# Low parts of weights written over the raw tiles in place, in a decoder trunk on one Trainium2 core

## The chip, the cores and the metric

The kernel runs on one core of one Trainium2 chip. The metric is device time in microseconds, lower is better; a run's time is that of the core. The engines named below are TensorE (PE, its weight loads PEld), VectorE (DVE), ScalarE (ACT), GpSimd (POOL) and SyncE (SP), which issues most DMA transfers.

## The reference

One layer of a decoder trunk on 256 positions of 2048 channels, in f32. The input is normalised, projected to seven widths of 1024 and three gates of 2048, and goes through three branches: a spatial-gating MLP (A), an S5 state-space layer with a GLU (B) and cross-attention into 256 memory tokens (X). Each is gated, projected back to 2048, weighed by a sigmoid gate and summed; an output projection, a norm and the residual follow.

```python
h = rms_norm(x, pre_g)
proj = h @ w_in
a_u, a_v, a_g, b_x, b_g, x_q, x_g, gate_logits = jnp.split(proj, splits, axis=-1)
y_a = spatial_gating(a_u, a_v, sg_ln_g, sg_ln_b, sg_w, sg_b) * jax.nn.silu(a_g)
y_b = s5_branch(b_x, ..., glu_w, glu_b) * jax.nn.silu(b_g)
y_x = memory_cross_attention(x_q, rms_norm(mem, mem_g), xa_wk, xa_wv) * jax.nn.silu(x_g)
branch = jnp.einsum('bsnc,ncd->bsnd', jnp.stack([y_a, y_b, y_x], axis=2), w_branch)
merged = jnp.sum(jax.nn.sigmoid(gate_logits) * branch, axis=2)
return x + rms_norm(merged @ w_out, post_g)
```

In the S5 branch the GLU is `y * sigmoid(y @ glu_w + glu_b)`, with `y` the GELU of the scan's output.

## The kernel before

Every large product is made of rounded f32 numbers in two parts: a weight `w` becomes a high part (a cast to the rounded type fp32r) and a low part (`w` minus the high part, rounded too), an activation likewise, and TensorE adds high x high, low x high and high x low. So each weight is loaded once, split once by a cast on ScalarE (L92) and a subtraction on VectorE (L93), and used by three groups of matmuls.

The weights come as 160 raw tiles of 128 partitions x 2048 f32 (1 MB each), numbered here from 0 in the order in which they are loaded: the S5 input (0 to 3), queries (4 to 11), keys, values, the X gate (28 to 35), the X merge with its gate logits and branch projection (36 to 59), A's three inputs, the A merge (84 to 107), B's gate (108 to 115), the gate logits of B (116 to 131), the GLU (132 to 135), the branch projection of B (136 to 143), and the output projection (144 to 159). A load is one DMA, issued by SP (`load`, L78), into one of three raw buffers. `split` (L85) cuts a tile in halves of 1024 columns: each takes one of four buffers `hl` of high and low part together. A raw buffer is free again when the second half has been subtracted, an `hl` buffer when TensorE has used it.

Two product forms use the tiles. `cm_block` has weights stationary (a tile is 16 blocks of 128 columns), `tm_quarter` has activations stationary and weights moving (a tile is 4 rows of 512). Results gather in two PSUM accumulators `acc`. An evacuation frees one: for the column form `fold` copies one half on ScalarE (L230) and adds the other on VectorE (L231). At the GLU (L904 to L919) a raw tile fills one accumulator, and its evacuation goes on with two sigmoids (ScalarE, L913), two products (VectorE, L915 and L916) and the split of two blocks `yB` (L92, L93), which the branch projection of B takes as stationary operand: tile 136 uses `yB` blocks 0 to 3, tile 137 blocks 4 to 7. In attention (L705 to L755), four heads share one PSUM buffer `misc` for scores `sc`, transposed probabilities `tp` (copied out by ScalarE, L734) and the output `po`.

The matmuls' order is the order in the code. The other engines get theirs from a scheduler, by due times and priorities: splits are raised by 250 steps (`AHEAD`), so that they come before evacuations; the S5 work (tables, scans, `E`, `p`, `s`) is fed in small steps between tiles by `pump`. Once built, each engine runs its list in order, and an instruction that waits holds all behind it.

Of the kernel before, what the change touches and what calls it, by code (L numbers as in the profile page):

```python
# [9 lines left out]
F32 = mybir.dt.float32  # L10
# [33 lines left out]
def trunk(ctx: ExitStack, tc: tile.TileContext, I, out):  # L44
    nc = tc.nc
    v, a, g, pe = nc.vector, nc.scalar, nc.gpsimd, nc.tensor

    xp = ctx.enter_context(tc.tile_pool(name="xp", bufs=1))
    xv = xp.tile([P, T + 48], F32, name="xv")
    const = ctx.enter_context(tc.tile_pool(name="const", bufs=1))  # L50
    big = ctx.enter_context(tc.tile_pool(name="big", bufs=1))
    rawp = ctx.enter_context(tc.tile_pool(name="rawp", bufs=3))
    hip = ctx.enter_context(tc.tile_pool(name="hip", bufs=4))
    wk = ctx.enter_context(tc.tile_pool(name="wk", bufs=2))
# [20 lines left out]

    def load(src):
        t = rawp.tile([P, 2048], F32, tag="raw", name=nm("raw"))
        nc.sync.dma_start(out=t, in_=src)  # L78
        return t

    def halves(off):
        t = hip.tile([P, 2 * 1024 + 128], F32R, tag="hl", name=nm("hl"))
        return t[:, off:off + 1024], t[:, off + 1024:off + 2048]

    def split(src, off=0):  # L85
        hi, lo = halves(off)
        with tc.high_priority(offset=AHEAD):
            split_to(hi, lo, src)
        return hi, lo
# [27 lines left out]
    const.tile([P, 32], F32, name="vpad")  # L117
    first = rawp.tile([P, 2, 768], F32, tag="raw", name="first", padded_shape=[P, 2, 1024])
    nc.sync.dma_start(out=xv, in_=I["xvecs"])
# [90 lines left out]
    def cm_block(ps, raw, hl, mm_=cm_mm):  # L210
        for hf in range(2):
            wh, wl = split(raw[:, hf * 1024:(hf + 1) * 1024], CM_OFF)
            for k in range(8):
                kk = hf * 8 + k
                mm_(ps, wh[:, k * P:(k + 1) * P], wl[:, k * P:(k + 1) * P], hl[kk], kk == 0, kk == 15)
            pump(rate["cm"])

    def tm_quarter(acc, raw, hl, kq, nk):
        for hf in range(2):
            wh, wl = split(raw[:, hf * 1024:(hf + 1) * 1024])  # L220
            for k in range(2):
                kk = kq * 4 + hf * 2 + k
                sl = slice(k * 512, (k + 1) * 512)
                for tb in range(2):
                    tm_mm(acc[tb], wh[:, sl], wl[:, sl], hl[kk], tb, kk == 0, kk == nk - 1)
            pump(rate["tm"])

# [6 lines left out]
    def cm_pairs(src, nblk, hl, evac, mm_=cm_mm):  # L234
        for bp in range(nblk // 2):
            ps = acc_tile()
            for b in range(2):
                cm_block(ps[:, b], load(src[2 * bp + b]), hl, mm_)
            evac(bp, ps)
# [10 lines left out]
    for pc in range(8):  # L250
        if pc == 0:
            raw = first
        elif pc < 3:
            raw = rawp.tile([P, 2, 768], F32, tag="raw", name=nm("st"), padded_shape=[P, 2, 1024])
        else:
            raw = slot(("H0", "H1", "H2", "H3", "M0")[pc - 3], [P, 2, 1024])[:, :, 0:768]
        wh, wl = (z.rearrange("p (q n) -> p q n", q=2) for z in halves(CM_OFF))
        parts = [slice(0, 1), slice(1, 2)]
        for q in parts if pc < 3 else [slice(0, 2)]:
            if pc > 0 or q.start > 0:  # L260
                nc.sync.dma_start(out=raw[:, q], in_=I["start"][pc][:, q])
# [509 lines left out]
    def merge(n, yhl, sink):  # L771
        for c in range(4):
# [212 lines left out]
    for kh in range(2):  # L985
        raw = load(I["w_out3"][0, kh])
        for hf in range(2):
            wh, wl = split(raw[:, hf * 1024:(hf + 1) * 1024])
            for k in range(4):
                for tb in range(2):  # L990
                    tm_k(acc[:, tb, 0:T], wh[:, k * T:(k + 1) * T], wl[:, k * T:(k + 1) * T], kh * 8 + hf * 4 + k, tb)
    for tb in range(2):
# [8 lines left out]
    for kh in range(2):  # L1001
        raw = load(I["w_out3"][1, kh])
        for hf in range(2):
            src = raw[:, hf * 1024:(hf + 1) * 1024]
            if kh == 0 and hf == 0:
                for i in range(2):
                    wh = s5p.tile([P, 512], F32R, tag="s", name=nm("wh"), bufs=4)
                    wl = s5p.tile([P, 512], F32R, tag="s", name=nm("wl"), bufs=4)
                    split_to(wh, wl, src[:, i * 512:(i + 1) * 512])
                    wks += [(wh[:, k * T:(k + 1) * T], wl[:, k * T:(k + 1) * T]) for k in range(2)]  # L1010
            else:
                wh, wl = split(src)
                wks += [(wh[:, k * T:(k + 1) * T], wl[:, k * T:(k + 1) * T]) for k in range(4)]
    at = [bup.tile([P, 512], F32, tag="bu", name=nm("oacc")) for _ in range(2)]
# [115 lines left out]
```

## Time and profile before

| | |
|---|---|
| median of 3 runs | 914.53 us (914.26 to 915.4) |
| the profiled execution | 915.75 us, of which 914.0 us lie between first and last instruction |
| granted TensorE clock | 0.999 |
| TensorE, VectorE, ScalarE busy | 900.7, 765.3, 560.0 us |
| HBM read, written | 190.39 MB, 2.10 MB (211 GB/s over the span) |

In rows of the profile a line like L93 is that of the helper; `hl` is a high and low buffer, `raw` a raw tile, `acc` an accumulator. A row of a group ends in its busy time and the mean of one, and after the second bar the idle time of the engine before these instructions, with what ended it. A row of the timeline begins with start and duration in us. A row of the waits gives the total, the number of times and the longest. Engines other than TensorE have idle time that costs nothing.

### The profile page before, as it was taken

What the parts mean: (1) busy time and instruction counts of PE and PEld (TensorE: products, weight loads), DVE (VectorE), ACT (ScalarE), POOL (GpSimd) and SP (SyncE); (2) the same over time, 40 slices, a digit from 0 to 9 for tenths busy, and PEclk for the clock granted to TensorE, in tenths of its full rate; (3) what the DMA queues carried; (4) which work ended last, traced back from release to release, by engine and by line L of the source; (5) the groups of instructions that cost most, each with busy time, mean ns of one, the idle gap of its engine ahead of it and who ended that gap; (6) DMA issues with size and microseconds to landing.
All of it is one profiled execution on the core that took longest, in us unless ns stands there. A gap on an engine that the chain in (4) does not pass through costs nothing.

```text
span 914.0 us, 12943 instructions
## 1 busy us (share of the span) xinstructions
PE 900.7 (99%) x4864; PEld 798.7 (87%) x4864; DVE 765.3 (84%) x1202; ACT 560.0 (61%) x962; POOL 22.4 (2%) x46
## 2 busy tenths in 40 slices
PE   8999999999999999999999999999999999999996
PEld 6999898889888888889999888888988889998896
DVE  6899967976779999999888799999997967876554
ACT  7575755755558677666454765777666647544452
POOL 1000000000000000000000000000000000000000
PEclk9999999999999999999999999999999999999999
DMA  9887565555454565655755556556655565657542
GB/s 350 303 309 295 219 231 190 196 189 191 147 205 167 200 232 211 235 188 189 257 182 207 177 176 223 186 199 222 213 190 210 195 236 203 216 185 276 197 172 93
DMA packets 30175, 193.33 MB, mean 212 GB/s; under 512 B 3744, under 2 KB 4128, under 8 KB 8352
## 3 DMA queue, kind: packets, MB, share of 16 engines
q1 hardware_dynamic: 28000, 186.08, 56.7%
q0 software_dynamic: 1536, 4.20, 1.4%
q10 hardware_dynamic: 576, 2.23, 0.7%
q8 instruction: 38, 0.62, 0.3%
q14 instruction: 25, 0.20, 0.1%
HBM read 190.39 MB, written 2.10 MB: 211 GB/s over the span
## 4 chain that ended last, share of the span: by engine, by line
PE 74%; DVE 17%; ACT 3%; issue 3%; DMA 1%; SPq 0%; DVEq 0%; ACTq 0%
PE acc L175 17%; PE acc L180 15%; PE acc L181 15%; PE acc L182 15%; PE acc L174 8%; DVE hl L93 6%; DVE p L371 2%; ACT hl L92 2%; DVE p L600 1%; DVE s L371 1%; PE y L624 1%; PE po L742 1%; DMA M<-memT 1%; DMA st<-start 1%; DVE q L371 1%
## 5 line engine op out<-in xcount | busy, mean ns | idle before, releaser
L93 DVE TENSOR_TENSOR hl<-raw,hl 128x1024 fp32r<-128x1024 f32 x319 | 388.6, 1221 | 112.0 <-ACT hl L92 110.5
L92 ACT CAST hl<-raw 128x1024 fp32r<-128x1024 f32 x319 | 330.7, 1045 | 200.0 <-PE acc L182 120.8
L175 PE MATMUL acc<-x,hl 128*128 128x512 f32 x736 | 241.6, 383 | 0.1
L174 PE MATMUL acc<-x,hl 128*128 128x256 f32 x690 | 189.1, 274 | 1.4 <-DVE hl L93 1.4
L180 PE MATMUL acc<-hl,x 128*128 128x512 f32 x448 | 171.5, 383 | 0.0
L181 PE MATMUL acc<-hl,x 128*128 128x512 f32 x448 | 169.9, 379 | 0.8 <-DVE hl L93 0.8
L182 PE MATMUL acc<-hl,x 128*128 128x512 f32 x448 | 169.8, 379 | 0.0
L175 PEld LDWEIGHTS acc<-x,hl 128*128 128x128 f32 x736 | 137.0, 190 | 18.1 <-ACT hl L92 1.0
L174 PEld LDWEIGHTS acc<-x,hl 128*128 128x128 f32 x690 | 132.3, 192 | 3.0 <-DVE hl L93 1.7
L180 PEld LDWEIGHTS acc<-hl,x 128*128 128x128 f32 x448 | 84.7, 189 | 14.1 <-issue 2.9
L181 PEld LDWEIGHTS acc<-hl,x 128*128 128x128 f32 x448 | 84.7, 189 | 12.4 <-DVE hl L93 1.2
L182 PEld LDWEIGHTS acc<-hl,x 128*128 128x128 f32 x448 | 84.7, 189 | 12.0
L180 PE MATMUL acc<-hl,H 128*128 128x512 f32 (+1 forms) x224 | 83.5, 373 | 0.0
L181 PE MATMUL acc<-hl,H 128*128 128x512 f32 (+1 forms) x224 | 83.2, 372 | 0.0
L182 PE MATMUL acc<-hl,H 128*128 128x512 f32 (+1 forms) x224 | 83.2, 372 | 0.0
L175 PE MATMUL acc<-H,hl 128*128 128x512 f32 x192 | 62.6, 382 | 0.0
L174 PE MATMUL acc<-H,hl 128*128 128x256 f32 x176 | 48.2, 274 | 0.2 <-DVE hl L93 0.2
L182 PEld LDWEIGHTS acc<-hl,H 128*128 128x128 f32 x224 | 42.4, 189 | 5.6
L181 PEld LDWEIGHTS acc<-hl,H 128*128 128x128 f32 x224 | 42.4, 189 | 5.4
L180 PEld LDWEIGHTS acc<-hl,H 128*128 128x128 f32 x224 | 42.4, 189 | 5.3
L371 DVE TENSOR_TENSOR p<-bu,E 128x512 f32<-128x512 f32 x64 | 41.9, 686 | 0.9 <-PE bu L562 0.7
L600 DVE TENSOR_TENSOR_SCAN p<-s5r,p 128x256 f32<-128x256 f32 x64 | 40.9, 680 | 0.6
(253 smaller groups left out, 1187.4 us busy)
## 6 DMA issues: line engine op xcount, KB each, us to landing
raw<-w_gate SPq DMA_DIRECT2D x48, 1024.0 KB, 4.8
raw<-w_br SPq DMA_DIRECT2D x24, 1024.0 KB, 4.7
raw<-w_out SPq DMA_DIRECT2D x16, 1024.0 KB, 4.8
raw<-w_xq SPq DMA_DIRECT2D x8, 1024.0 KB, 4.9
raw<-wk SPq DMA_DIRECT2D x8, 1024.0 KB, 4.7
raw<-wv SPq DMA_DIRECT2D x8, 1024.0 KB, 4.8
raw<-w_xg SPq DMA_DIRECT2D x8, 1024.0 KB, 4.7
raw<-w_av SPq DMA_DIRECT2D x8, 1024.0 KB, 4.8
```

What stands on the lines that cost most here:

```text
L92: a.copy(out=hi, in_=src)
L93: v.tensor_tensor(out=lo, in0=src, in1=hi.bitcast(F32), op=ALU.subtract)
L174: pe.matmul(ps[:, 0:T], lhsT=wl, rhs=hl.moving(0), start=False, stop=False)
L175: pe.matmul(ps, lhsT=wh, rhs=hl.moving_both(), start=first, stop=last)
L180: pe.matmul(ps, lhsT=hl.stationary(0, tb), rhs=two(wh), start=first, stop=False)
L181: pe.matmul(ps, lhsT=hl.stationary(0, tb), rhs=two(wl), start=False, stop=False)
L182: pe.matmul(ps, lhsT=hl.stationary(1, tb), rhs=two(wh), start=False, stop=last)
L371: v.tensor_tensor(out=o, in0=i0, in1=i1, op=op)
L600: v.tensor_tensor_scan(out=p2[:, ri], data0=rb, data1=p1[:, ri], initial=0.0, op0=ALU.mult, op1=ALU.add)
L624: pe.matmul(ps[32 * j:32 * j + 32, :], lhsT=cbt[:, cb * 4 + j, ri, :], rhs=ss[j][:, ri, :], start=ri == 0, stop=ri == 1, tile_position=(0, ...
L742: pe.matmul(po[:, c, :], lhsT=vv[:, mb, (2 * h + c) * P:(2 * h + c + 1) * P], rhs=pT[:, h, mb, :], start=mb == 0, stop=mb == 1)
```

## The change

A raw tile now becomes its own low part. There are four buffers, each seen by two names, `raw` (f32) and `low` (fp32r), at one address; three `hl` buffers hold the 2048 high columns of a whole tile. `split` makes two casts of 1024 columns, as before, and then one subtraction of 2048 columns that writes the low part over the raw tile. So a raw buffer is free when TensorE has used it, and SP's loads wait for TensorE where they waited for VectorE. In column form a tile is placed 352 bytes further in, as the `hl` buffers were. The start pieces use the same buffers; their splits keep their sizes. The gate sigmoids `sg` of the merges move from a work pool to free slots (X0, H0). The last output tile, whose first half was split in quarters into small buffers, is split like the others. What each product computes is the same.

```diff
--- before.py
+++ after.py
@@ -35,6 +35,8 @@
 BEHIND = 0
 NWARM = 8
 CM_OFF = 352 // 4
+NRAW = 4
+RW = 2048 + 128
 RT = (0.66, 0.8, 0.47, 0.62, 0.58, 0.55, 1.32)
 GELU_S = 2.0 * math.sqrt(2.0 / math.pi)
 GELU_C = 0.044715
@@ -45,12 +47,16 @@
     nc = tc.nc
     v, a, g, pe = nc.vector, nc.scalar, nc.gpsimd, nc.tensor
 
+    at0 = nc.sbuf_base
+    nc.alloc_sbuf_tensor("arena", [P, NRAW * RW + 128], F32)
+    at0 += (320 - at0) % 512
+    raws = [nc.alloc_sbuf_tensor_at(f"raw{i}", [P, RW], F32, offset=at0 + i * RW * 4).ap() for i in range(NRAW)]
+    lows = [nc.alloc_sbuf_tensor_at(f"low{i}", [P, RW], F32R, offset=at0 + i * RW * 4).ap() for i in range(NRAW)]
     xp = ctx.enter_context(tc.tile_pool(name="xp", bufs=1))
     xv = xp.tile([P, T + 48], F32, name="xv")
     const = ctx.enter_context(tc.tile_pool(name="const", bufs=1))
     big = ctx.enter_context(tc.tile_pool(name="big", bufs=1))
-    rawp = ctx.enter_context(tc.tile_pool(name="rawp", bufs=3))
-    hip = ctx.enter_context(tc.tile_pool(name="hip", bufs=4))
+    hip = ctx.enter_context(tc.tile_pool(name="hip", bufs=3))
     wk = ctx.enter_context(tc.tile_pool(name="wk", bufs=2))
     s5p = ctx.enter_context(tc.tile_pool(name="s5p", bufs=2))
     s5c = ctx.enter_context(tc.tile_pool(name="s5c", bufs=1))
@@ -73,19 +79,32 @@
         s = nm("sm")
         return const.tile(shape, dt, tag=s, name=s)
 
-    def load(src):
-        t = rawp.tile([P, 2048], F32, tag="raw", name=nm("raw"))
-        nc.sync.dma_start(out=t, in_=src)
-        return t
+    turn = [0]
+
+    def next_raw():
+        turn[0] += 1
+        return (turn[0] - 1) % NRAW
+
+    def load(src, off=0):
+        i, sl = next_raw(), slice(off, off + 2048)
+        nc.sync.dma_start(out=raws[i][:, sl], in_=src)
+        return raws[i][:, sl], lows[i][:, sl], off
+
+    def high(off):
+        return hip.tile([P, RW], F32R, tag="hl", name=nm("hl"))[:, off:off + 2048]
 
     def halves(off):
-        t = hip.tile([P, 2 * 1024 + 128], F32R, tag="hl", name=nm("hl"))
-        return t[:, off:off + 1024], t[:, off + 1024:off + 2048]
-
-    def split(src, off=0):
-        hi, lo = halves(off)
+        t = high(off)
+        return t[:, 0:1024], t[:, 1024:2048]
+
+    def split(raw):
+        src, lo, off = raw
+        hi = high(off)
         with tc.high_priority(offset=AHEAD):
-            split_to(hi, lo, src)
+            for hf in range(2):
+                sl = slice(hf * 1024, (hf + 1) * 1024)
+                a.copy(out=hi[:, sl], in_=src[:, sl])
+            v.tensor_tensor(out=lo, in0=src, in1=hi.bitcast(F32), op=ALU.subtract)
         return hi, lo
 
     def split_to(hi, lo, src):
@@ -115,7 +134,10 @@
     a.activation(out=warm, in_=warm, func=AF.Exp)
     vecs = xv[:, T:T + 48]
     const.tile([P, 32], F32, name="vpad")
-    first = rawp.tile([P, 2, 768], F32, tag="raw", name="first", padded_shape=[P, 2, 1024])
+    def raw_piece():
+        return raws[next_raw()][:, 0:1536].rearrange("p (q n) -> p q n", q=2)
+
+    first = raw_piece()
     nc.sync.dma_start(out=xv, in_=I["xvecs"])
     nc.scalar.dma_start(out=first[:, 0, T:T + 256], in_=I["start"][0][:, 0, T:T + 256])
     nc.sync.dma_start(out=first[:, 0, T + 256:768], in_=I["start"][0][:, 0, T + 256:768])
@@ -208,22 +230,21 @@
     rate = {"cm": 0.62, "tm": RT[6]}
 
     def cm_block(ps, raw, hl, mm_=cm_mm):
-        for hf in range(2):
-            wh, wl = split(raw[:, hf * 1024:(hf + 1) * 1024], CM_OFF)
-            for k in range(8):
-                kk = hf * 8 + k
-                mm_(ps, wh[:, k * P:(k + 1) * P], wl[:, k * P:(k + 1) * P], hl[kk], kk == 0, kk == 15)
-            pump(rate["cm"])
+        wh, wl = split(raw)
+        for k in range(16):
+            mm_(ps, wh[:, k * P:(k + 1) * P], wl[:, k * P:(k + 1) * P], hl[k], k == 0, k == 15)
+            if k % 8 == 7:
+                pump(rate["cm"])
 
     def tm_quarter(acc, raw, hl, kq, nk):
-        for hf in range(2):
-            wh, wl = split(raw[:, hf * 1024:(hf + 1) * 1024])
-            for k in range(2):
-                kk = kq * 4 + hf * 2 + k
-                sl = slice(k * 512, (k + 1) * 512)
-                for tb in range(2):
-                    tm_mm(acc[tb], wh[:, sl], wl[:, sl], hl[kk], tb, kk == 0, kk == nk - 1)
-            pump(rate["tm"])
+        wh, wl = split(raw)
+        for k in range(4):
+            kk = kq * 4 + k
+            sl = slice(k * 512, (k + 1) * 512)
+            for tb in range(2):
+                tm_mm(acc[tb], wh[:, sl], wl[:, sl], hl[kk], tb, kk == 0, kk == nk - 1)
+            if k % 2:
+                pump(rate["tm"])
 
     def fold(ps, bc):
         t = wk.tile([P, 2, T], F32, tag="w0", name=nm("f"))
@@ -235,7 +256,7 @@
         for bp in range(nblk // 2):
             ps = acc_tile()
             for b in range(2):
-                cm_block(ps[:, b], load(src[2 * bp + b]), hl, mm_)
+                cm_block(ps[:, b], load(src[2 * bp + b], CM_OFF), hl, mm_)
             evac(bp, ps)
 
     wz = wk.tile([P, 512], BF16, tag="w1", name="wz", padded_shape=[P, 1024])
@@ -251,7 +272,7 @@
         if pc == 0:
             raw = first
         elif pc < 3:
-            raw = rawp.tile([P, 2, 768], F32, tag="raw", name=nm("st"), padded_shape=[P, 2, 1024])
+            raw = raw_piece()
         else:
             raw = slot(("H0", "H1", "H2", "H3", "M0")[pc - 3], [P, 2, 1024])[:, :, 0:768]
         wh, wl = (z.rearrange("p (q n) -> p q n", q=2) for z in halves(CM_OFF))
@@ -776,7 +797,9 @@
                 tm_quarter([G[:, 0], G[:, 1]], load(I["w_gate"][n, c, kq]), xhl, kq, 16)
             assert not bg[2]
             Bp = acc_tile()
-            sg = wk.tile([P, 2, 512], F32, tag="w0", name=nm("g"))
+            if c == 0:
+                sgs = slot("X0" if n == 2 else "H0", [P, 2, 2, 512])
+            sg = sgs[:, c % 2]
             for tb in range(2):
                 a.activation(out=sg[:, tb], in_=G[:, tb], func=AF.Sigmoid, scale=rstd_x[:, tb:tb + 1])
             for kq in range(2):
@@ -903,9 +926,9 @@
         yB += [s5p.tile([P, 2, T], F32R, tag=tag, name=nm("yB"), bufs=n) for _ in range(n)]
     for bp in range(4):
         ps = acc_tile()
-        raw = load(I["glu"][bp])
+        gh, gw = (z.rearrange("p (b n) -> p b n", b=2) for z in split(load(I["glu"][bp], CM_OFF)))
         for b in range(2):
-            wh, wl = split(raw[:, b * 1024:(b + 1) * 1024], CM_OFF)
+            wh, wl = gh[:, b], gw[:, b]
             for k in range(8):
                 cm_mm(ps[:, b], wh[:, k * P:(k + 1) * P], wl[:, k * P:(k + 1) * P], ygl[k], k == 0, k == 7)
         t = fold(ps, None)
@@ -999,18 +1020,8 @@
 
     wks = []
     for kh in range(2):
-        raw = load(I["w_out3"][1, kh])
-        for hf in range(2):
-            src = raw[:, hf * 1024:(hf + 1) * 1024]
-            if kh == 0 and hf == 0:
-                for i in range(2):
-                    wh = s5p.tile([P, 512], F32R, tag="s", name=nm("wh"), bufs=4)
-                    wl = s5p.tile([P, 512], F32R, tag="s", name=nm("wl"), bufs=4)
-                    split_to(wh, wl, src[:, i * 512:(i + 1) * 512])
-                    wks += [(wh[:, k * T:(k + 1) * T], wl[:, k * T:(k + 1) * T]) for k in range(2)]
-            else:
-                wh, wl = split(src)
-                wks += [(wh[:, k * T:(k + 1) * T], wl[:, k * T:(k + 1) * T]) for k in range(4)]
+        wh, wl = split(load(I["w_out3"][1, kh]))
+        wks += [(wh[:, k * T:(k + 1) * T], wl[:, k * T:(k + 1) * T]) for k in range(8)]
     at = [bup.tile([P, 512], F32, tag="bu", name=nm("oacc")) for _ in range(2)]
     ro = small([P, 2])
     ms = small([P, 2])
...
```

The hunks left out give the column loads of `w_bx` their offset and write the output projection's split as one call for a tile.

The matmuls stand in the same order. On VectorE 1202 instructions become 1042, and what stands between them moves. VectorE at the GLU, before: the sum of an accumulator (L231) for tile 132, half subtractions of the next tiles (`hl`), products, and the `yB` low parts.

```order
L93 TENSOR_TENSOR hl_7231<-raw_7210,hl_7231 128x1024
L231 TENSOR_TENSOR f_7146<-acc_7105,f_7146 128x512
L93 TENSOR_TENSOR hl_7264<-raw_7262,hl_7264 128x1024
L915 TENSOR_TENSOR f_7146<-f_7146,U_129 128x512
L916 TENSOR_TENSOR f_7146<-f_7146,X_788_5937 128x512
L93 TENSOR_TENSOR hl_7283<-raw_7262,hl_7283 128x1024
L93 TENSOR_TENSOR yB_7097<-f_7146,yB_7097 128x256
L93 TENSOR_TENSOR yB_7098<-f_7146,yB_7098 128x256
L231 TENSOR_TENSOR f_7198<-acc_7157,f_7198 128x512
```
The same place now (L252 is the sum, L107 the subtraction of a whole tile, L938 and L939 the products, L112 the `yB` low parts; `low_61` is tile 135, `low_62` tile 136):

```order
L107 TENSOR_TENSOR low_61<-raw_57,hl_6854 128x2048
L252 TENSOR_TENSOR f_6743<-acc_6705,f_6743 128x512
L938 TENSOR_TENSOR f_6743<-f_6743,U_133 128x512
L939 TENSOR_TENSOR f_6743<-f_6743,X_564_5609 128x512
L107 TENSOR_TENSOR low_62<-raw_58,hl_6903 128x2048
L112 TENSOR_TENSOR yB_6697<-f_6743,yB_6697 128x256
L112 TENSOR_TENSOR yB_6698<-f_6743,yB_6698 128x256
L252 TENSOR_TENSOR f_6792<-acc_6754,f_6792 128x512
```
Before, `raw_7262` is tile 135: the sum of tile 132 stood ahead of its two halves and that of tile 133 right behind them. Now the sum of tile 132 has all of tile 135 ahead of it, and that of tile 133 all of tile 136.

ScalarE there, before, from the second cast of tile 135 on:

```order
L92 CAST hl_7283<-raw_7262 128x1024
L92 CAST yB_7097<-f_7146 128x256
L92 CAST yB_7098<-f_7146 128x256
L230 COPY f_7198<-acc_7157 128x512
L92 CAST hl_7316<-raw_7314 128x1024
L913 ACTIVATE f_7198<-f_7198,xv 128x256 x2
L92 CAST hl_7331<-raw_7314 128x1024
```
And now, from the casts of tile 136 on:

```order
L106 CAST hl_6903<-raw_58 128x1024 x2
L111 CAST yB_6697<-f_6743 128x256
L111 CAST yB_6698<-f_6743 128x256
L251 COPY f_6792<-acc_6754 128x512
L106 CAST hl_6932<-raw_55 128x1024 x2
L936 ACTIVATE f_6792<-f_6792,xv 128x256 x2
L251 COPY f_6841<-acc_6803 128x512
```
The copy of tile 133's accumulator (`f_7198`) stood ahead of the first cast of tile 136 (`raw_7314`), the sigmoids between that tile's two casts; now the copy (`f_6792`) stands behind both casts of tile 136, and its sigmoids behind both of tile 137.

ScalarE in attention, between the copy of the S5 base `E` and the copy of the first head's transposed probabilities `tp`, before:

```order
L541 COPY E_2644<-ebase 128x2x32
L549 ACTIVATE t_2650<-E_2644,pwr 128x32
L550 ACTIVATE t_2650<-E_2644,pwr 128x32
L92 CAST hl_2084<-raw_2060 128x1024
L230 COPY f_1995<-acc_1884 128x512
L734 COPY H_195_1883<-tp_1988 128x512
```
And now:

```order
L562 COPY E_2520<-ebase 128x2x32
L570 ACTIVATE t_2526<-E_2520,pwr 128x32
L106 CAST hl_2020<-raw_58 128x1024 x2
L251 COPY f_1907<-acc_1802 128x512
L755 COPY H_137_1801<-tp_1900 128x512
```
Between the two copies stood one cast of a weight and now there are two.

More of the change, by code (lines that the diff above doesn't have):

```diff
@@ L345, in trunk @@
     b45 = [bup.tile([P, 512], F32, tag="bu", name=f"bx{i}") for i in (4, 5)]
-    cm_block(b45[0], load(I["w_bx"][0]), xhl)
+    cm_block(b45[0], load(I["w_bx"][0], CM_OFF), xhl)
     for i in range(2):
         fold_u(u[:, 2 * i:2 * i + 2, :], acc0[i])
-    cm_block(b45[1], load(I["w_bx"][1]), xhl)
+    cm_block(b45[1], load(I["w_bx"][1], CM_OFF), xhl)
     ps = acc_tile()
-    cm_block(ps[:, 0], load(I["w_bx"][2]), xhl)
+    cm_block(ps[:, 0], load(I["w_bx"][2], CM_OFF), xhl)
     for i in range(2):
@@ L356, in trunk @@
         nc.sync.dma_start(out=Cin[i], in_=I["s5c"][:, i])
-    cm_block(ps[:, 1], load(I["w_bx"][3]), xhl)
+    cm_block(ps[:, 1], load(I["w_bx"][3], CM_OFF), xhl)
     fold_u(u[:, 6:8, :], ps)
@@ L985, in trunk @@
     for kh in range(2):
-        raw = load(I["w_out3"][0, kh])
-        for hf in range(2):
[L988 to L991, printed above, removed]
+        wh, wl = split(load(I["w_out3"][0, kh]))
+        for k in range(8):
+            for tb in range(2):
+                tm_k(acc[:, tb, 0:T], wh[:, k * T:(k + 1) * T], wl[:, k * T:(k + 1) * T], kh * 8 + k, tb)
     for tb in range(2):
@@ L1001, in trunk @@
     for kh in range(2):
-        raw = load(I["w_out3"][1, kh])
-        for hf in range(2):
-            src = raw[:, hf * 1024:(hf + 1) * 1024]
-            if kh == 0 and hf == 0:
-                for i in range(2):
-                    wh = s5p.tile([P, 512], F32R, tag="s", name=nm("wh"), bufs=4)
-                    wl = s5p.tile([P, 512], F32R, tag="s", name=nm("wl"), bufs=4)
-                    split_to(wh, wl, src[:, i * 512:(i + 1) * 512])
-                    wks += [(wh[:, k * T:(k + 1) * T], wl[:, k * T:(k + 1) * T]) for k in range(2)]
-            else:
-                wh, wl = split(src)
-                wks += [(wh[:, k * T:(k + 1) * T], wl[:, k * T:(k + 1) * T]) for k in range(4)]
+        wh, wl = split(load(I["w_out3"][1, kh]))
+        wks += [(wh[:, k * T:(k + 1) * T], wl[:, k * T:(k + 1) * T]) for k in range(8)]
     at = [bup.tile([P, 512], F32, tag="bu", name=nm("oacc")) for _ in range(2)]
```

## The prediction

> **What bounds the kernel now.** I read the page's busy lines first, then its chain, then the groups, then the list of waits.
>
> ```profile
> PE 900.7 (99%) x4864; PEld 798.7 (87%) x4864; DVE 765.3 (84%) x1202; ACT 560.0 (61%) x962; POOL 22.4 (2%) x46
> PE 74%; DVE 17%; ACT 3%; issue 3%; DMA 1%; SPq 0%; DVEq 0%; ACTq 0%
> L93 DVE TENSOR_TENSOR hl<-raw,hl 128x1024 fp32r<-128x1024 f32 x319 | 388.6, 1221 | 112.0 <-ACT hl L92 110.5
> L92 ACT CAST hl<-raw 128x1024 fp32r<-128x1024 f32 x319 | 330.7, 1045 | 200.0 <-PE acc L182 120.8
> L175 PE MATMUL acc<-x,hl 128*128 128x512 f32 x736 | 241.6, 383 | 0.1
> ```
>
> TensorE is busy 99% of the 914.0 us and almost never waits. The weight splits (L93, L92) are the largest groups of VectorE and ScalarE, yet both engines wait there for work: ScalarE 120.8 us for a matmul that frees a buffer, VectorE 110.5 us for ScalarE's cast. Only what stops TensorE can be won, and the list of waits has nearly all of it:
>
> ```profile
> PEld acc L174 <- DVE hl L93: 2.5, 3, 1.7
> PE acc L174 <- DVE hl L93: 1.6, 2, 1.4
> PE sc L711 <- ACT H L734: 1.4, 1, 1.4
> PE acc L181 <- DVE hl L93: 0.8, 1, 0.8
> ...
> 10.25 0.38 PE L174 MATMUL acc<-x,hl 128*128 128x256 f32 x1 [1.44 <-DVE hl L93]
> 99.59 0.38 PE L175 MATMUL acc<-H,hl 128*128 128x512 f32 x1
> 100.15 0.38 PE L174 MATMUL acc<-H,hl 128*128 128x256 f32 x1 [0.17 <-DVE hl L93]
> 609.83 0.38 PE L180 MATMUL acc<-hl,x 128*128 128x512 f32 x1
> 610.98 0.48 PE L181 MATMUL acc<-hl,x 128*128 128x512 f32 x1 [0.77 <-DVE hl L93]
> ```
>
> The list's 1.4 us of L174 lie at 10.25 us, before the first weights, in the start pieces, whose splits keep their sizes; they stay. The other places show how late a matmul starts: with 0.22 us from one matmul of 512 columns to the next, 100.15 is 0.34 late and 610.98 is 0.93 late, and the scores of L711 wait 1.4. That is 2.7 us; with the short pauses within 1 us of them I put what a faster split could win at 3.5 us at the most (an estimate).
>
> **The change, part by part.**
>
> *Fewer, longer subtractions.* 319 of 1024 columns become 160 of 2048. No row has 2048 columns; bounds come from these:
>
> ```profile
> 30.46 2.36 DVE L93 TENSOR_TENSOR hl<-raw,hl 128x1024 fp32r<-128x1024 f32 x2 [0.26 <-ACT hl L92]
> L371 DVE TENSOR_TENSOR p<-bu,E 128x512 f32<-128x512 f32 x64 | 41.9, 686 | 0.9 <-PE bu L562 0.7
> ```
>
> Above: two alone, 2 x 1.221 = 2.44 us. Below: 686 ns at 512 and 1221 at 1024 make 535 ns for each 512, so 1.221 + 1.070 = 2.29 us. I take 2.29. Per tile VectorE gains 0.15 us against separate halves, but 0.07 against the back-to-back pair of the row (2.36); over 160 tiles that is 11 to 24 us of its 765, on an engine which is idle 16% of the span. On TensorE's path that gain is worth nothing: the cover is the 5.2 us that one tile's matmuls take (below). Without that cover it would be up to 0.15 us a tile.
>
> [...]
>
> *Buffers and loads.* A raw tile is now freed by the last matmul on it, not by its second subtraction. Four buffers let the load of a tile start when TensorE ends the fourth tile before it.
>
> ```profile
> raw<-w_gate SPq DMA_DIRECT2D x48, 1024.0 KB, 4.8
> 777.33 0.38 PE L180 MATMUL acc<-hl,yB 128*128 128x512 f32 x1
> 780.35 0.38 PE L182 MATMUL acc<-hl,yB 128*128 128x512 f32 x1
> 782.51 0.38 PE L180 MATMUL acc<-hl,yB 128*128 128x512 f32 x1
> ```
>
> A tile lasts 782.51 - 777.33 = 5.18 us, so the load has three tiles, 15.5 us, less 4.8 to land. The high buffer (three now) comes free two tiles ahead, 10.4 us; two casts (2 x 1.045) and one subtraction (2.29) take 4.4, so both halves are ready about 6.0 us early. In steady state nothing stalls, and SP's loads standing behind a matmul cost 0. Where VectorE was backlogged by the state-space work (94 to 100 and 611 us), its order now puts that tile's subtraction several us of work earlier, so I take its 1.3 us of lateness (0.34 + 0.93) with the pauses beside it: -2.0 (bounds 0, and -2.1 of the 3.5 once the 1.4 of the scores is out).
>
> *Evacuations stand behind whole tiles.* ScalarE and VectorE run in program order, and splits are put ahead of the rest. Where an evacuation used to come between two halves, it now waits for two casts (2.1 us) and then for 2.29 us, not for half of each. Most have a tile or two of slack. At the GLU and the projection after it they have none. VectorE, ScalarE and TensorE of before there:
>
> ```profile
> 761.81 1.05 ACT L92 CAST hl<-raw 128x1024 fp32r<-128x1024 f32 x1 [1.53 <-PE acc L175]
> 762.76 0.58 ACT L230 COPY f<-acc 128x512 f32<-128x512 f32 x1
> 765.38 0.90 ACT L913 ACTIVATE f<-f,xv 128x256 f32<-128x256 f32 x2
> 768.15 0.71 ACT L92 CAST yB<-f 128x256 fp32r<-128x256 f32 x2
> 767.37 0.69 DVE L916 TENSOR_TENSOR f<-f,X 128x512 f32<-128x512 f32 x1
> 770.00 0.68 DVE L231 TENSOR_TENSOR f<-acc,f 128x512 f32<-128x512 f32 x1
> 774.53 0.76 DVE L93 TENSOR_TENSOR yB<-f,yB 128x256 fp32r<-128x256 f32 x2
> 784.94 0.75 DVE L93 TENSOR_TENSOR yB<-f,yB 128x256 fp32r<-128x256 f32 x2
> 771.87 0.60 PE L175 MATMUL acc<-H,hl 128*128 128x512 f32 x2
> 785.53 0.38 PE L182 MATMUL acc<-hl,yB 128*128 128x512 f32 x1
> ```
>
> Tile numbers count loads: 132 to 135 are the GLU, 136 and 137 the first projection tiles. I play the new order by hand on the old TensorE clock, with these durations. Tile 135 starts at 772.09 (the second matmul of the 771.87 row) if the sum of tile 133's accumulator (L231, ended 770.68) has freed it: 1.4 us of slack. Now: casts of 135 end at 763.8, its subtraction at 766.1, the sum of 132 at 766.7, the sigmoids at 767.6, the two products at 769.05; casts of 136 to 769.6, its subtraction to 771.9, two yB subtractions to 772.5, and only then the sum of 133, to 773.15. Tile 135 starts at 773.2: **+1.1**. Next: casts of 137 to 774.3, sigmoids of 133, copy of 134 to 775.6, subtraction of 137 to 776.6, product, sum of 134 and product to 778.35, its sigmoids to 778.7, its products to 780.15; casts of 138 to 780.7, subtraction to 782.95, first yB low of block 2 at 783.3. Tile 136, started at 778.45, wants it 780.35 - 777.33 = 3.02 us in, at 781.5: **+1.8**. It ends at 785.45, which frees the buffer for tile 139's casts (to 787.8); the subtraction ends at 790.05 and the yB low of block 6 at 790.4. Tile 137 wants that at 785.45 + 3.02 = 788.5: **+1.9**. Sum **+4.8 us**. In the old trace the same operand was ready about 785.35 for a matmul at 785.53, so almost no slack was there. Bounds: 0, if every added wait falls into slack, and 6.8, three times one more cast and half subtraction (3 x 2.27).
>
> *Attention.* The second scores wait for one PSUM buffer, which ScalarE's copy of the transposed probabilities frees.
>
> ```profile
> 188.53 1.22 DVE L93 TENSOR_TENSOR hl<-raw,hl 128x1024 fp32r<-128x1024 f32 x1
> 191.26 0.68 DVE L371 TENSOR_TENSOR s<-p,E 128x512 f32<-128x512 f32 x1
> 191.98 0.25 ACT L541 COPY E<-ebase 128x64 f32<-128x64 f32 x1 [3.10 <-DVE s L371]
> 192.69 1.03 ACT L92 CAST hl<-raw 128x1024 fp32r<-128x1024 f32 x1
> 194.11 0.58 ACT L734 COPY H<-tp 128x512 f32<-128x512 f32 x1
> 194.74 2.00 PE L711 MATMUL sc<-M,X 128*128 128x256 f32 x8 [1.42 <-ACT H L734]
> ```
>
> Before, one cast stood between the E copy and that copy; now two do (+0.95), and the E copy waits for an `s` product that stands behind a whole subtraction (+1.0, less what the two half ones around it gave back). The copy ends near 196.4 and the scores start 1.7 us later: **+1.7** (bounds -0.2, if the relieved VectorE is early, and +2.1, a cast and half a subtraction). The other three heads have slack of about what one cast adds: 0.
>
> *The rest.* The sigmoid gates move to free slots of the same form, and the last projection tile no longer splits in quarters; both end well before TensorE wants them: 0. Start and tail keep their work: 0.
>
> *Sum.* 915.75 (the profiled execution, 1.75 around its span) - 2.0 + 4.8 + 1.7 = 920.25. The median of the runs shown is 1.2 under the profiled time, so I predict **919.0 us**.
>
> **The rivals.**
>
> *No change.* The GLU slack absorbs the order: ScalarE's queue shifts so that evacuations run in the 1.53 us idle spells, as the row at 761.81 shows one. Then -2.0 and about +2 swap: 914.5. For it: both engines are idle often. Against it: the order is fixed, an idle spell before a cast can't be used by a sum behind it.
>
> *Faster.* VectorE is what matters wherever it is the releaser (17% of the chain). Its 11 to 24 us come off ahead of the stalled places, the three stalls go whole (-3.5) and the GLU sums still arrive inside their 1.4 us: 914.53 - 3.5 + at most 1 = 911.0 to 912.0. It decides if the chain of sums at the GLU comes out 1 us earlier than played. [...] Against it: the subtraction before a sum is longer than the old half by 1.07 us, five times in a row.
>
> *Slower still.* Loads wait for matmuls, and where extra megabytes share the queue the lead goes:
>
> ```profile
> M<-memT SPq DMA_DIRECT2D x2, 1024.0 KB, 7.5
> M<-mem SPq DMA_DIRECT2D x2, 1024.0 KB, 6.7
> ACT wh L92 <- DMA raw<-w_out: 0.8, 1, 0.8
> ```
>
> With one such megabyte ahead the landing takes 4.8 + 7.5 = 12.3 of the 15.5 us, leaving 3.2 where the two casts and the subtraction want 4.4: 1.2 us late against the first matmul, up to four times between 37 and 90 us. It decides from a landing of 11.1 us on. Then 919.0 + 3 to 5 = 922 to 924. Against it: the waits of before have no load as releaser of a weight cast beyond one of 0.8 us.
>
> **How the numbers follow.** This kernel's measurement can't tell a change within 0.2%, or 1.8 us. My forecast (916.4 to 921.5) has 0.50, no change 0.25 (912.7 to 916.4), faster 0.13, slower still 0.12. So faster 0.13, same 0.25, slower 0.62. The likeliest case's own range is 916.4 to 921.5; the range for 8 in 10 takes in no change and most of the others' near ends: 912.3 to 922.8.
>
> **What would show it.** A group of 160 subtractions of about 2.29 us, and VectorE busy 11 to 24 us less. No L174 or L181 wait on a split at 94 to 100 and 611 us. `sc` waits of about 3 us behind the copy of `tp`. Three new gaps of TensorE between 765 and 795 us: one before the last GLU tile, released by the sum of an accumulator, and two inside the first projection tiles, released by yB subtractions, 4.8 us together. I am wrong if these gaps are missing, if a matmul waits for a raw load, or if gaps appear in steady tiles far from any evacuation.

## The result and the profile after

The changed kernel takes 930.44 us (median; 930.12 to 931.39), the kernel before beside it 915.17 (914.26 to 915.53): ratio 1.0169, 95% interval 1.0159 to 1.0179, so 15.3 us slower. The profiled execution took 930.12 us, with a span of 928.4.

The page of the changed kernel, busy time, chain and the two split groups:

```profile
PE 904.5 (97%) x4864; PEld 798.6 (86%) x4864; DVE 751.8 (81%) x1041; ACT 546.3 (59%) x961; POOL 23.4 (3%) x46
...
PE 66%; DVE 22%; ACT 7%; issue 4%; DMA 0%; DVEq 0%; SPq 0%; ACTq 0%
...
L107 DVE TENSOR_TENSOR low<-raw,hl 128x2048 fp32r<-128x2048 f32 x160 | 365.8, 2288 | 130.8 <-ACT hl L106 130.7
L106 ACT CAST hl<-raw 128x1024 fp32r<-128x1024 f32 x320 | 318.1, 1043 | 176.2 <-PE acc L204 101.9
```

VectorE did get lighter, by 13.5 us (765.3 to 751.8), and one subtraction takes 2288 ns where 2.29 us was reckoned. Yet VectorE's and ScalarE's shares of the chain rise from 20% to 29%: TensorE waits for them more often. The list of waits names for whom:

```profile
PE sc L732 <- ACT H L755: 4.9, 1, 4.9
PE acc L204 <- DVE yB L112: 3.3, 2, 1.6
PE acc L197 <- DVE f L252: 2.2, 2, 1.2
PE acc L199 <- DVE low L107: 2.1, 3, 1.1
```

Both kernels issue the same 4864 matmuls in the same order, so the start of each can be set beside its start before. How much later than before TensorE is, added in each stage (times of the kernel before; worked out from the two traces):

| stage, us | added |
|---|---|
| start pieces, S5 input, first queries, 0 to 60 | -0.8 |
| queries, keys, 60 to 110 | 0.0 |
| keys, values, 110 to 188 | +0.8 |
| second scores and what follows, 188 to 207 | +5.3 |
| the other heads, 207 to 250 | +1.1 |
| X merge, w_av, 250 to 400 | +0.1 |
| A's inputs, 400 to 445 | +3.5 |
| A merge, 600 to 640 | -1.0 |
| GLU and projection, 760 to 795 | +5.3 |
| all other stages | 0.0 |
| sum | +14.4 |

The sum is the difference of the spans. The first row arises in the start pieces, before 11 us, and varies between executions: the traces of three versions below that are the same kernel up to there (halves at the GLU, halves in attention, 20 extra matmuls) have -0.25, -0.15 and -0.47. The gaps themselves on TensorE, rows of the timeline of the changed kernel (in brackets the idle time before the row and what ended it):

```profile
81.31 0.38 PE L199 MATMUL acc<-x,low 128*128 128x256 f32 x1 [0.61 <-DVE low L107]
119.25 0.38 PE L199 MATMUL acc<-H,low 128*128 128x256 f32 x1 [0.34 <-DVE low L107]
198.50 0.49 PE L732 MATMUL sc<-M,X 128*128 128x256 f32 x1 [4.94 <-ACT H L755]
422.76 0.38 PE L199 MATMUL acc<-x,low 128*128 128x256 f32 x1 [1.12 <-DVE low L107]
440.23 0.48 PE L197 MATMUL acc<-x,hl 128*128 128x512 f32 x1 [1.22 <-DVE f L252]
782.36 0.48 PE L197 MATMUL acc<-H,hl 128*128 128x512 f32 x1 [0.93 <-DVE f L252]
792.61 0.49 PE L204 MATMUL acc<-hl,yB 128*128 128x512 f32 x1 [1.65 <-DVE yB L112]
799.79 0.49 PE L204 MATMUL acc<-hl,yB 128*128 128x512 f32 x1 [1.65 <-DVE yB L112]
```

There are two kinds. Some matmuls wait for a low part (`low`), others for an evacuation (`f`, `yB`, the copy `H` of the transposed probabilities) that stands behind whole-tile splits. The second kind, at the GLU, on VectorE and ScalarE:

```profile
778.74 2.29 DVE L107 TENSOR_TENSOR low<-raw,hl 128x2048 fp32r<-128x2048 f32 x1 [0.47 <-ACT hl L106]
780.95 0.76 DVE L112 TENSOR_TENSOR yB<-f,yB 128x256 fp32r<-128x256 f32 x2
781.62 0.69 DVE L252 TENSOR_TENSOR f<-acc,f 128x512 f32<-128x512 f32 x1
...
787.90 1.99 ACT L106 CAST hl<-raw 128x1024 fp32r<-128x1024 f32 x2
789.80 1.32 ACT L111 CAST yB<-f 128x256 fp32r<-128x256 f32 x4
...
789.93 2.29 DVE L107 TENSOR_TENSOR low<-raw,hl 128x2048 fp32r<-128x2048 f32 x1 [0.55 <-ACT hl L106]
792.14 1.42 DVE L112 TENSOR_TENSOR yB<-f,yB 128x256 fp32r<-128x256 f32 x4
```

The sum of tile 133 ends at 782.3 behind tile 136's subtraction, and the matmul starts at 782.36; the `yB` low parts come at 792.1 behind tile 138's.

### The profile page after: what moved, and what is told of

Read it like the earlier page. It is cut to its first block, busy times and chain, and to the rows that moved or that the text cites. A ratio compares the mean times of both kernels' runs of the same rounds, so it can differ in the third digit from the quotient of the medians.

```text
span 928.4 us, 12843 instructions
## 1 busy us (share of the span) xinstructions
PE 904.5 (97%) x4864; PEld 798.6 (86%) x4864; DVE 751.8 (81%) x1041; ACT 546.3 (59%) x961; POOL 23.4 (3%) x46
## 3 DMA queue, kind: packets, MB, share of 16 engines
q1 hardware_dynamic: 28000, 186.08, 55.7%
## 4 chain that ended last, share of the span: by engine, by line
PE 66%; DVE 22%; ACT 7%; issue 4%; DMA 0%; DVEq 0%; SPq 0%; ACTq 0%
PE acc L197 15%; PE acc L202 13%; PE acc L204 13%; PE acc L203 13%; DVE low L107 10%; PE acc L196 7%; ACT hl L106 5%; DVE p L392 3%; DVE p L621 2%; PE sc L732 1%; PE po L763 1%; DVE B L553 1%; PE y L645 1%; DVE H L191 1%; DVE E L395 1%
## 5 line engine op out<-in xcount | busy, mean ns | idle before, releaser
L107 DVE TENSOR_TENSOR low<-raw,hl 128x2048 fp32r<-128x2048 f32 x160 | 365.8, 2288 | 130.8 <-ACT hl L106 130.7
L196 PE MATMUL acc<-x,low 128*128 128x256 f32 x630 | 172.9, 274 | 0.0
L202 PE MATMUL acc<-hl,x 128*128 128x512 f32 x448 | 171.5, 383 | 0.0
L203 PE MATMUL acc<-low,x 128*128 128x512 f32 x448 | 170.0, 379 | 0.0
L204 PE MATMUL acc<-hl,x 128*128 128x512 f32 x448 | 169.8, 379 | 0.0
L197 PEld LDWEIGHTS acc<-x,hl 128*128 128x128 f32 x736 | 136.8, 190 | 19.3 <-DVE f L252 1.5
L196 PEld LDWEIGHTS acc<-x,low 128*128 128x128 f32 x630 | 121.1, 192 | 1.1
L202 PEld LDWEIGHTS acc<-hl,x 128*128 128x128 f32 x448 | 84.7, 189 | 14.1 <-issue 2.9
L204 PEld LDWEIGHTS acc<-hl,x 128*128 128x128 f32 x448 | 84.7, 189 | 12.0
L203 PEld LDWEIGHTS acc<-low,x 128*128 128x128 f32 x448 | 84.7, 189 | 11.7 <-DVE low L107 0.5
L202 PE MATMUL acc<-hl,H 128*128 128x512 f32 (+1 forms) x224 | 83.5, 373 | 0.0
L203 PE MATMUL acc<-low,H 128*128 128x512 f32 (+1 forms) x224 | 83.2, 372 | 0.0
L204 PE MATMUL acc<-hl,H 128*128 128x512 f32 (+1 forms) x224 | 83.2, 372 | 0.0
L576 ACT COPY E<-E 128x256 f32<-128x256 f32 x32 | 12.9, 404 | 54.5 <-DVE E L395 54.3
```

Source lines behind the costliest of these rows:

```text
L107: v.tensor_tensor(out=lo, in0=src, in1=hi.bitcast(F32), op=ALU.subtract)
L196: pe.matmul(ps[:, 0:T], lhsT=wl, rhs=hl.moving(0), start=False, stop=False)
L197: pe.matmul(ps, lhsT=wh, rhs=hl.moving_both(), start=first, stop=last)
L202: pe.matmul(ps, lhsT=hl.stationary(0, tb), rhs=two(wh), start=first, stop=False)
L203: pe.matmul(ps, lhsT=hl.stationary(0, tb), rhs=two(wl), start=False, stop=False)
L204: pe.matmul(ps, lhsT=hl.stationary(1, tb), rhs=two(wh), start=False, stop=last)
```

## The experiments

My theory after the comparison: the loss lies in what stands behind a whole-tile split in an in-order queue. Rivals: buffers that are freed late, the long instruction as such at every tile, S5 work that is late in any form.

**1. Halves again, everywhere, then at single places.** In `split`, a tile in a set CUT has its second cast and subtraction issued where they stood before:

```diff
+        cut = ntile[0] in CUT
...
+        def half(hf):
+            sl = slice(hf * 1024, (hf + 1) * 1024)
+            with tc.high_priority(offset=AHEAD):
+                a.copy(out=hi[:, sl], in_=src[:, sl])
+                v.tensor_tensor(out=lo[:, sl], in0=src[:, sl], in1=hi[:, sl].bitcast(F32), op=ALU.subtract)
...
+        if cut:
+            half(0)
+            return hi, lo, lambda: half(1)
```

All tiles:

> The changed kernel with every subtraction cut in two again (1024 columns each, the second half issued where it stood before); low parts still go over the raw tiles, loads still wait for TensorE, three high buffers. Theory (whole-tile splits are what evacuations and S5 steps queue behind): the 15 us go, 914 to 916 us, no gap of TensorE at the last GLU tile, scores' wait back to 1.4 to 2 us. Rival (buffers: a raw tile is held until TensorE is done, so loads and casts come late): 925 us or more, and the same gaps.

Measured 916.54 us against 915.34 (ratio 1.0019, 1.001 to 1.0029). Some 14 us are gone with the buffers, loads behind TensorE and low parts in place unchanged: the late-buffer rival falls. The scores' wait was 2.3 us, above the 1.4 to 2 that I expected. In this trace TensorE's last matmul starts 0.7 us earlier than before, yet the span is 0.25 longer: the last write of the output landed 3.5 us after its issue, in the kernel before 2.5. Four of its ten runs took 917.8 to 918.7 us; the trace is of one of the other six, which all lie below 916.8 (last section).

Tiles 132 to 139:

> The changed kernel with two half subtractions for tiles 132 to 139 alone (GLU and the projection after it). Theory: the three gaps there (1.1, 1.8, 1.8 us and the slower matmul after each, 5.1 us together) go and nothing else: 930.4 - 5.1 = 925.3 us. Rival (the gaps come from buffers that are free later): 930 us.

Measured 925.45 (ratio 1.0112). The three gaps are gone, 5.0 us, as expected, and no other stage moved by more than 0.6 us.

Tiles 28 to 35:

> The changed kernel with two half subtractions for tiles 28 to 35 alone (attention). Theory: the wait of the second scores falls from 4.9 to between 1.4 and 2.5 us, the granted clock stays at 1.0 behind it, and with the 0.7 us at the later heads the time is 930.4 - 5 = 925 to 926 us. Rival (the wait comes from ScalarE's S5 casts of that place, which stand ahead of the split in either form): a wait of 4 us or more, 929 to 931 us.

Measured 927.68 (ratio 1.0132), only 2.8 us better. The wait fell to 2.56 us, between the theory (at most 2.5) and the rival (4 or more), and a slow clock still followed (0.50 from 199 to 201 us; experiment 4 and the last section), so the time missed the expected 925 to 926.

41 tiles at the four places:

> The changed kernel with two half subtractions in 41 tiles alone: 8 to 19 (queries and keys, beside the S5 tables), 28 to 35 (attention), 66 to 78 (A's inputs, beside the S5 steps and the layer norm), 132 to 139 (GLU and projection); the other 119 stay whole. Theory: all of the loss lies at these places, so the time comes back to that of the kernel with all halves, 916.5 us, within 1.5. Rival (whole-tile splits or late buffers cost a little at each of 160 tiles): 920 us or more.

Measured 917.59 (ratio 1.0026, 1.0017 to 1.0035), 1.1 above all halves and within the margin stated. 119 whole subtractions of 2.29 us cost nothing or close to it; the loss is local.

**2. The order, with whole subtractions kept.**

```diff
-AHEAD = 250
+AHEAD = 20
```

> The changed kernel with splits raised by 20 steps instead of 250, so that evacuations stand ahead of more of them; all instructions keep their size. If the place in the order is the cause and not the length of one instruction: the sum of the GLU's accumulator and the scores' copy come earlier, the gaps at the GLU shrink by 3 us or more, 920 to 926 us, unless splits now come late elsewhere. If the length is the cause: within 2 us of 930.4.

Measured 918.85 (ratio 1.004, 1.0025 to 1.0055): 11.6 us back with no instruction cut, more than the range that I gave. GLU, A's inputs and the scores together cost 0.4 us more than before; instead splits come late at 83 to 127 us (+2.2 between 60 and 180) and at 375 (+1.9). Then, with AHEAD back at 250, the evacuations alone were raised (`fold`, the GLU's sigmoids, products and yB splits, the copy of `tp`):

```diff
-        a.copy(out=t, in_=ps[:, :, T:2 * T])
-        v.tensor_tensor(out=t, in0=ps[:, :, 0:T], in1=t, op=ALU.add)
+        with tc.high_priority(offset=400):
+            a.copy(out=t, in_=ps[:, :, T:2 * T])
+            v.tensor_tensor(out=t, in0=ps[:, :, 0:T], in1=t, op=ALU.add)
...
```

> The changed kernel with its 160 whole subtractions, but with the evacuations that TensorE waits for raised above the splits: the two halves of each accumulator's sum, the GLU's sigmoids, products and yB splits, and the copy of the transposed probabilities. If the place in the queue is the cause: the accumulator sums at 440 and 782 us come 2 to 3 us earlier and those gaps go, the yB gaps shrink to 1 us together, the scores wait 1 to 2 us less; 930.4 - 7 = 923 us, 921 to 925. If a subtraction of 2.29 us is too long wherever it stands: within 2 us of 930.4.

Measured 921.31 (ratio 1.0065, 1.005 to 1.0081), inside the expected range. The list of waits of this run:

```profile
PE acc L199 <- DVE low L107: 3.4, 4, 1.1
PE sc L733 <- ACT H L757: 3.0, 1, 3.0
```

`f` and `yB` are gone from it, and GLU and projection cost 0.0 instead of 5.3 us. But the gap at 440 us did not go: at 437.9 TensorE waits there for a low part instead, and A's inputs still cost 3.4. So the place in the queue is shown for the GLU; at A's inputs the first kind of wait was under it.

**3. What the low part itself costs.** To take the scores out of the picture, the evacuations of `fold_u` were raised too, and the scores of heads 1 to 3 and the outputs of all four heads put half a tile later among the matmuls:

```diff
-        for _ in range(4 * h):
+        for _ in range(4 * h + (h > 0)):
...
-        for _ in range(h):
+        for _ in range(h + 1):
```

> The changed kernel with its 160 whole subtractions and the same two edits. Theory: what is left of its loss are the waits for a whole low part beside the S5 steps (81, 119, 420, 431, 438 us, 5 us) with the scores' wait and the slow clock behind it gone: 921.3 - 3 = 918 us, 917 to 919.5. If the long subtraction costs at every tile: 920 or more.

Measured 917.87 (ratio 1.0027, 1.0016 to 1.0037), as expected. The scores wait 0.4 us now, and 3.4 of the remaining loss lie at A's inputs. There in this run:

```profile
415.95 0.38 PE L199 MATMUL acc<-x,low 128*128 128x256 f32 x1 [1.12 <-DVE low L107]
```

> The last kernel with whole subtractions (917.9 us), with two half subtractions in the five tiles alone whose first low-part matmul waited there: 10, 17, 69, 71 and 72 (1.0, 0.3, 1.3, 0.3 and 1.2 us); 155 stay whole. Theory (what waits is the first half's low part, which one long subtraction gives 1.1 us later): 917.9 - 4.1 = 913.8 us, 913 to 915.2. Rival (VectorE's backlog is what makes them late, in either form, or the wait moves to the next tile): 916 us or more.

Measured 915.72 (ratio 1.0004, 0.9995 to 1.0014), between theory and rival. All five gaps went (4.1 us in the two traces), but tile 16 now waits 0.3 us at 113 us, and at A's inputs there is a gap that was not there:

```profile
436.38 0.38 PE L213 MATMUL acc<-x,low 128*128 128x256 f32 x1 [1.35 <-DVE low L121]
```

This is tile 73, still whole. A first half that is ready 1.1 us earlier does help, and VectorE's backlog there (layer norm and scans) hands 1.5 us of it on to the next whole tile. Both are at work; how much is each was not separated.

**4. The slow clock behind the long wait.** In the changed kernel the eight score matmuls after the wait start 0.43 us apart, before 0.22. Stretches of the kernel before, of the changed one, and of the one with 20 extra matmuls (columns: stretch, length, busy time and count of PE, PEld, DVE, ACT, POOL, granted clock, DMA share, GB/s; 1.00 is full speed):

```profile
200.00:202.00 2.00, 2.00 (x15) 1.84 (x14) 1.47 (x2) 0.46 (x1) 0.00 (x0) 1.00 0.00 0
```
```profile
194.00:198.00 4.00, 0.00 (x0) 0.00 (x0) 2.15 (x4) 2.96 (x6) 0.00 (x0) 1.00 0.00 0
200.00:202.00 2.00, 2.00 (x7) 1.65 (x6) 1.26 (x4) 0.00 (x0) 0.00 (x0) 0.50 0.00 0
```

```diff
+        if h == 1:
+            fill = yp.tile([P, 512], F32, tag="y", name=nm("fill"))
+            for _ in range(20):
+                pe.matmul(fill, lhsT=xhl[0].stationary(0, 0), rhs=xhl[0].moving_both(), start=True, stop=True)
```

> The changed kernel with 20 matmuls of 512 columns that nobody reads put on TensorE where it waits for the second scores (4.3 us of work in a wait of 4.9). Theory (a wait of 5 us lowers the granted clock for some 4 us behind it, at a price of 1.5 us): the granted clock stays 1.0 and the matmuls after the wait start 0.22 us apart, 930.4 - 1.5 = 929 us. Rival (the matmuls behind the wait are slow since scores are reads of wide f32 operands): the time stays at 930.4 or rises.

```profile
194.00:198.00 4.00, 4.00 (x19) 3.21 (x17) 2.14 (x4) 2.79 (x5) 0.00 (x0) 1.00 0.01 2
200.00:202.00 2.00, 2.00 (x14) 1.83 (x13) 1.98 (x4) 0.00 (x0) 0.00 (x0) 1.00 0.03 8
```

Measured 929.0 us (ratio 1.0153, 1.0136 to 1.017), as expected: matmuls that nobody reads save 1.4 us, since the clock stays up (1.00 from 200 to 202 us, in the changed kernel 0.50). The two ratios' intervals overlap, but all four runs lie below all six of the changed kernel.

**5. Is writing in place worth something by itself?** In halves over the raw tiles with the evacuations raised:

> All subtractions in halves over the raw tiles, and the same evacuations raised. Theory: TensorE's scores wait at 194 us falls from 2.4 to about 1.4 us and nothing else changes: 915.5 us, 914 to 916.5, level with the kernel before. If raising them delays splits, new waits on a split appear and it is 917 us or more.

914.46 (ratio 0.9991, 0.9981 to 1.0), level with the kernel before or a little under. With the edits of the scores and `fold_u` as well:

> All halves over the raw tiles, evacuations raised (the sums of the column form at queries and keys too), and the scores and outputs of heads 1 to 3 placed half a tile later among the matmuls. Theory: the scores' wait of 1.5 us at 194 us and the wait of 0.76 at 114 us go, TensorE's work elsewhere is the same: 914.5 - 2.2 = 912.3 us, 911.5 to 913.5. If the copy that the scores wait for is late by more than half a tile: 913.5 or more.

913.7 (ratio 0.9981, 0.9972 to 0.999). TensorE no longer waits for the scores, but low parts came late at 119.8 and 126.1 us (0.4 and 1.0), so the gain was 0.8 and not 2.2, and the time is just above the 913.5 that I gave as the limit. The same two edits on the kernel before, with its own buffers:

> The kernel before with the same two edits (evacuations raised, scores half a tile later), its own buffers and low parts beside the high parts. It tells what writing in place is worth by itself once the order is the same. Theory (in place is worth the gaps at 100 and 611 us and a little at the start, 1 to 2 us): 915.3 - 1.6 = 913.7 us, 1 to 2 us above the in-place version. Rival (in place is worth nothing): level with it.

913.39 (ratio 0.9977, 0.9968 to 0.9986): faster than both kernels, and level with the in-place version (0.3 us apart, the intervals overlap). My expectation that in place would be 1 to 2 us ahead was wrong; the rival, that it is worth nothing, holds. In place does away with the late split at 611 us, which stays here,

```profile
608.55 0.48 PE L181 MATMUL acc<-hl,x 128*128 128x512 f32 x1 [0.77 <-DVE hl L93]
```

and loses as much beside the keys, where its first low parts come late (+1.6 us from 110 to 180 us, in this version 0.0).

## Why the prediction was wrong

The sum added 4.5 us to the time before, the spans differ by 14.4. Of the 9.9 us between them, attention holds 4.8, A's inputs 3.5, the credit for splits that come earlier 1.8 and the GLU 0.5; the start gives 0.8 back.

*Right.* TensorE bounds the kernel (97% busy); a subtraction of 2048 columns costs 2.29 us; VectorE gains 11 to 24 us (13.5 measured) and this is worth nothing on TensorE's path (917.59 us with 119 whole subtractions, 916.54 with none); the 611 us wait goes (-1.0). Above all the GLU: worked out were +1.1, +1.8 and +1.9 us at the last GLU tile and the two projection tiles, measured steps of 1.09, 1.81 and 1.81, with 0.1 us at each for the slower matmul behind the gap (0.32 to 0.33 us to the next start for 0.22); the whole stage 5.3 against 4.8.

*Wrong: "Most have a tile or two of slack."* Only the GLU was played through. A's inputs were not, and cost 3.5 us that stand nowhere in the sum. There VectorE has S5 steps, the layer norm and the evacuations in one queue. In the changed kernel:

```profile
418.51 1.27 DVE L621 TENSOR_TENSOR_SCAN p<-s5r,p 128x256 f32<-128x256 f32 x2
419.82 0.69 DVE L392 TENSOR_TENSOR p<-p,E 128x512 f32<-128x512 f32 x1
420.43 2.28 DVE L107 TENSOR_TENSOR low<-raw,hl 128x2048 fp32r<-128x2048 f32 x1
...
434.88 2.49 DVE L392 TENSOR_TENSOR H<-H,X 128x512 f32<-128x512 f32 x4
437.29 2.28 DVE L107 TENSOR_TENSOR low<-raw,hl 128x2048 fp32r<-128x2048 f32 x1
439.49 0.68 DVE L252 TENSOR_TENSOR f<-acc,f 128x512 f32<-128x512 f32 x1
```

The subtraction at 420.43 starts behind a scan and a product, and its first half would have been done at 421.65 (1.22 us on); the whole is done at 422.7, and the matmul at 422.76 needs only the first half. At 439.49 an accumulator's sum comes behind four layer-norm steps and a whole tile.

*Wrong: the -2.0 for stages where VectorE is backlogged.* I reasoned that the subtraction now stands earlier in the order. It does, and at 100 and 611 us the waits went (-0.3 and -0.9, a little more with the matmul behind). But the first half is ready only with the second, which brought new waits at 81 and 119 us (+0.8 and +0.5). So the credit was right at two places beside S5 steps and had the wrong sign at two others; in the three rows concerned it came to -0.2 us. "Steady state" was right for most of the kernel: from 250 to 400, 445 to 600 and 640 to 760 us 0.1 us was added in all, although 48 of the 64 S5 scans run there. So S5 steps beside a tile are not enough for a wait. The new waits for a low part all lie in column form (L199); what else sets those tiles apart was not followed up.

*Mis-sized: attention, +1.7.* The mechanism, a copy behind two casts and an E copy behind a subtraction, is what the trace shows; it cost 6.5 us up to 250 us:

```profile
183.87 2.29 DVE L107 TENSOR_TENSOR low<-raw,hl 128x2048 fp32r<-128x2048 f32 x1 [1.44 <-ACT hl L106]
186.08 0.28 DVE L395 SCALAR_TENSOR_TENSOR E<-E,pwr,t 128x64 f32<-128x64 f32 x1
186.39 0.35 ACT L570 ACTIVATE t<-E,pwr 128x64 f32<-128x64 f32 x1 [0.69 <-DVE E L395]
186.65 0.39 ACT L552 CAST B<-sb 128x256 fp32r<-128x256 f32 x1
187.06 0.82 ACT L556 CAST U<-uhl 32x256 fp32r<-32x256 f32 x2
189.60 1.99 ACT L106 CAST hl<-raw 128x1024 fp32r<-128x1024 f32 x2
192.09 2.29 DVE L107 TENSOR_TENSOR low<-raw,hl 128x2048 fp32r<-128x2048 f32 x1
194.29 0.68 DVE L392 TENSOR_TENSOR s<-p,E 128x512 f32<-128x512 f32 x1
195.00 0.24 ACT L562 COPY E<-ebase 128x64 f32<-128x64 f32 x1 [2.69 <-DVE s L392]
195.51 1.97 ACT L106 CAST hl<-raw 128x1024 fp32r<-128x1024 f32 x2
197.87 0.58 ACT L755 COPY H<-tp 128x512 f32<-128x512 f32 x1
```

I started the first pair of casts from the old time. In the kernel before it ran behind ScalarE's S5 casts of `B` and `U` too, but earlier:

```profile
183.97 0.39 ACT L531 CAST B<-sb 128x256 fp32r<-128x256 f32 x1
186.88 1.99 ACT L92 CAST hl<-raw 128x1024 fp32r<-128x1024 f32 x2
```

Now ScalarE's row at 186.39 waits for the S5 step `E` (186.08), which stands on VectorE behind a whole subtraction; the casts of `B` and `U` and the pair follow it. So the pair began 2.7 us later and ran to 191.6. The copy at 195.00 then held ScalarE for 2.69 us until the `s` product, with the next pair (195.51) and the copy of `tp` (197.87) behind it in the order of the list, and the chain ended at 198.4 instead of 196.4: +2.0 us, and the wait was 4.9 us where about 3 were expected. The slow clock that followed (0.50 from 198.95 to 202.36 us) added 1.5, which no term held. The other heads, put at 0, cost 1.1.

*The rival "slower still"* gave 922 to 924 for loads that come late; loads were not the cause. ScalarE's casts of weights did wait for them, 11.5 us in all against 1.5 before, but with halves everywhere they waited 9.5 us and the loss was gone; and no TensorE wait has a load as releaser. The upper bound fell short since it was made of the places that I had listed, not of all places where a queue got coarser. No term of the sum stood for what shorter instructions on VectorE are worth to TensorE: cutting the subtractions again gave 13.9 us back, with VectorE busy 84% of the span of the kernel before.

## What to carry to other kernels

These rules are drawn from one kernel. On an engine that works in program order, as VectorE and ScalarE do in these traces, the size of the largest instruction ahead of others is a delay for all that queue behind it (here 2.29 us, before 1.22), and merging two halves also withholds the first half until the second is done (here 1.1 us); merge only where the consumer has the slack: whole subtractions cost 1.1 us at 119 tiles (917.59 against 916.54) and 12.9 at the other 41 (930.44 against 917.59). When a change makes a queue coarser, play the order through at every place where the consumer had less slack than the added length, not at the worst one alone. An evacuation that frees an accumulator or feeds the next matmul belongs ahead of a prefetching split: raising it, and placing a dependent matmul half a tile later, took 2 us off a kernel that was at 99% of TensorE (913.39 against 915.42), with no buffer changed.

## What was not expected of the hardware

TensorE's granted clock fell to 0.50 for 3.4 us, from 198.95 to 202.36, behind a single wait of 4.94 us in an otherwise busy stretch, which cost 1.5 us on top of the wait. A wait of 2.56 us was followed by a slow clock in one run (halves in attention) and not in another (halves at four places):

```profile
196.95 0.49 PE L750 MATMUL sc<-M,X 128*128 128x256 f32 x1 [2.56 <-ACT H L773]
```
```profile
195.18 0.49 PE L750 MATMUL sc<-M,X 128*128 128x256 f32 x1 [2.56 <-ACT H L773]
```

The stretches around and behind the two waits, in the same order (columns as in experiment 4):

```profile
197.00:199.00 2.00, 2.00 (x9) 1.73 (x9) 1.97 (x4) 1.05 (x1) 0.00 (x0) 0.82 0.00 0
199.00:201.00 2.00, 2.00 (x8) 1.72 (x7) 1.45 (x3) 0.42 (x2) 0.00 (x0) 0.50 0.03 8
```
```profile
195.00:197.00 2.00, 1.82 (x9) 1.68 (x9) 1.97 (x4) 1.17 (x2) 0.00 (x0) 1.00 0.00 0
197.00:199.00 2.00, 2.00 (x14) 1.82 (x13) 1.69 (x3) 0.19 (x1) 0.00 (x0) 1.00 0.04 8
```

So in these two traces it is not the length of a wait alone that decides; what else does was not shown. The times of one kernel also spread with the clock: with halves at four places, five runs took 916.1 to 917.1 us at a mean clock of 0.997 or 0.998 and five 918.0 to 919.4 at 0.996, so that the medians of that version and of all halves hold some of each kind.
